# Two gate groups per one-hot instruction, and new homes for the raw chunks of the U table

## The chip, the core and the metric

The kernel runs on one core of one Trainium2 chip. Its engines work side by side, each on its own queue of instructions, and wait for each other by semaphores: TensorE (PE, the matmuls), VectorE (DVE), ScalarE (ACT), GpSimd (POOL) and SyncE (SP, which here only issues transfers). The metric is the device time of one execution in microseconds (us).

## The reference, cut to what matters

The program is one layer of a decoder for 512 tokens of width 1024. A token mixer (Mamba-2 heads beside latent attention, one output projection, a layer norm) comes first and takes the first 390 us. The change lies in what follows, the PEER expert mixer:

```python
def block(xb):                                            # 128 tokens; 4 blocks
    q = (xb @ w_query).reshape(T, 8, 2, 128)
    s = einsum('thkd,hknd->thkn', q, sub_keys)            # scores of 2 x 128 sub-keys per head
    sv, si = top_k(s, 16)
    cand_s = sv[:, :, 0, :, None] + sv[:, :, 1, None, :]  # 256 candidates per head
    top_s, top_pos = top_k(cand_s, 16)
    expert_idx = take(si0 * 128 + si1, top_pos)           # 16 of 16,384 experts per head
    gate = softmax(top_s)
    act = gelu(einsum('td,thkd->thk', xb, u_table[expert_idx]))
    return einsum('thk,thkd->td', gate * act, v_table[expert_idx])
```

then a second layer norm. Each token picks 8 x 16 experts.

## The kernel before

**Dense instead of gathered.** For 352 tokens the kernel does not fetch the chosen rows. It multiplies the tokens with all 16,384 rows of U, in 128 chunks of 128 experts (`u_chunk`, two `step_u` halves of 12 matmuls each; L77 to L79 are the three products of half-precision high and low parts), takes the gelu of each chunk (`act`, L1543), multiplies it by a dense gate matrix G that is zero for the experts not chosen, and multiplies the result with all rows of V. 128 of block 3's and 32 of block 2's tokens are done by gathered rows instead (`row`, L1786, and `urow`, L1302).

**U's chunks.** Each 512 KB chunk is loaded raw by SP (`loads16`, L116), its squares are summed on ACT (`square`, L126, tile `jk`), a tiny matmul and three small ACT steps make a scale from it (`bound`, L132 to L135; for two chunks at a time while the chunk's number f is under FB), ACT writes the high part (`his`, L171), DVE or POOL the low part (`splits`, L191 to L193). Raw chunks lie in a ring of seven buffers: four named `ur`, three in V's low-part buffers `wil`, as long as V's own loads (`wir`) have not begun. The first 18 or so of these chunks are the 16 of `w_query`.

**Routing.** `stage2` computes scores, two top-16 searches per head on DVE, and in `routes` the softmax (an Exp on ACT, L1241) and the digits of the chosen keys (L1254 to L1262). ACT has to load another function table for Exp and again for gelu.

**G (build_g, L1390 to L1488).** 48 gate groups n: three blocks of 128 tokens, 16 groups each. `hot(n)` makes two one-hot arrays on DVE: `oj` (L1403, 128 x 1024) and `gi` (L1406, 128 x 2048, with the gates in it), from digits made every four groups (L1386 to L1388). 16 matmuls (L1433) turn them into G's slices in four PSUM banks, two ACT copies (L1435) put them into `stg`, and every four groups two stores on ACT's queue write them out: `gs0`, 128 KB, and `gsp`, 1920 KB. `oj` and `gi` have two buffers each; `hot(n+1)` is written while the matmuls of n run. Between the groups stand U half-chunks (`step_u`), and in groups 1 to 32 one dot each for the gathered U rows: L1308 on DVE multiplies a gathered row by the token and sums it; then POOL issues the gather of the row three further on (L1302, ring of three `urow` buffers). The order is that of the program text: each engine runs its own instructions as they were issued.

**V.** From chunk 54 on U and V chunks alternate; V's matmuls are L1721, L1722 and L1725, G's slices come back by `gt<-gsp` (L1658).

The change touches `loads16`, `square`'s order in `tick` and `bounds`, `routes`, `hot` and `build_g`, the loop of the output projection after L1470, `u_halves` (L1526) and the step from `build_g` to V (L1650 to L1680).

Of the kernel before, what the change touches and what calls it, by code (L numbers as in the profile page):

```python
# [11 lines left out]
F32 = mybir.dt.float32  # L12
# [37 lines left out]
FB = 72  # L50
# [8 lines left out]
def tile_block(ctx: ExitStack, tc: tile.TileContext, I, out):  # L59
# [25 lines left out]
    class Stream:  # L85
        def __init__(self, p, name, srcs, shape, raw=2, la=1, lo=None, bufs=None):
# [6 lines left out]
            self.sc, self.inv, self.by, self.nq, self.nb = {}, {}, {}, 0, 0  # L93
# [46 lines left out]
        def bounds(self, p, ps):  # L140
            f = self.nb
            if f < len(self.f16) and self.nq > f + (f < FB) and p >= f - ({4: 1, 6: 2, 8: 3}.get(f, 4) if f < FB else 2):
                self.bound(ps())

        def tick(self, p):
            while self.nq < len(self.f16):
                f = self.nq
                if p < ({4: 1, 5: 1, 6: 2, 7: 3, 8: 3, 9: 4}.get(f, f - 6) if f < FB else f - 3.5):
                    break
# [10 lines left out]
        def his(self, m):  # L160
            while self.nh < min(m, len(self.srcs)):
                n = self.nh
                if n in self.fi:
                    if not self.on:
# [15 lines left out]
        def splits(self, m):  # L180
            while self.ns < min(m, len(self.srcs)):
# [5 lines left out]
                if n in self.fi:  # L187
# [7 lines left out]
                    self.loads16(max(min(f + 8, FB), f + 5))  # L195
# [1008 lines left out]
    def routes(pl, ts, po, ti_, nb, nh, dst, after=lambda i: None, room=None, mid2=lambda i: None):  # L1204
# [35 lines left out]
        V.tensor_tensor(ab(1), v4(pf), v4(b1), op=OP.add)  # L1240
        A.activation(f4(d), f4(d), AF.Exp)  # L1241
        yield 0.8 + n * 0.0042
        V.tensor_reduce(sm, g4(d), axis=AX.X, op=OP.add)
        V.reciprocal(sm, sm)
        for i in range(nb):
            V.tensor_tensor(dst(i)[:, 2], d[:, i], sm[:, i * nh:(i + 1) * nh, None].to_broadcast([128, nh, 16]), op=OP.mult)
        yield 0.5 + n * 0.002
        sh = [128, 2 * nh, 16, 16]
        for i in order:
# [9 lines left out]
            yield 0.15 + nh * 0.27  # L1259
            mid2(i)  # L1260
# [131 lines left out]
    def build_g():  # L1392
        def hot(n):
# [3 lines left out]
            if n % 4 == 3:  # L1397
                DG.pop(n - 3)
# [4 lines left out]
            V.tensor_tensor(oj, iotaE[:, None].to_broadcast(bc),  # L1403
                            jT[:, g * 8:g * 8 + 8].rearrange("p (q c) -> p q c", c=2)[:, :, None, :].to_broadcast(bc),
                            op=OP.is_equal)
            V.tensor_tensor(gi.rearrange("p q a e b c -> p (q a) (e b) c"),  # L1406
                            hi[:, q0:q0 + 4].rearrange("p q a c -> p (q a) c")[:, :, None, :].to_broadcast([128, 64, 16, 2]),
# [602 lines left out]
```

## Time and profile before

| | us |
|---|---|
| three runs | 1550.53, 1550.50, 1549.11; median 1550.5 |
| profiled execution, its own time | 1550.87 |
| its span in the trace | 1549.1 (1.8 of the execution lie outside) |
| PE busy in the span | 1519.1 (98%) |
| DVE, ACT, POOL busy | 1346.3, 932.8, 508.1 |

The span runs from the first instruction to the last. PE's busy time is made of matmuls that overlap, so "98%" says that it was seldom without a matmul, not that each ran at its best. The trace names a wait by the engine that waited, what it had to start, and the instruction that released it; stretches below are given in us from the span's start.

### The profile page before, as it was taken

Reading aid. Unit: us, or ns where it says so; the run is one execution under the profiler, and the core shown is the slowest. Engines: PE = TensorE matmul, PEld = TensorE weight load, DVE = VectorE, ACT = ScalarE, POOL = GpSimd, SP = SyncE. Lnnn points to the kernel's source line nnn. Section 1 sums busy time; section 2 is a strip of 40 time slices with the busy share of each in tenths; the row PEclk is TensorE's granted clock in tenths of the full one; section 3 lists DMA queues with packets and bytes.
Section 4 is the critical chain, followed back from the end, with each engine's and each line's share of the span. In section 5 each row is a group of like instructions: output and inputs, shape, how many; then the busy total and the mean of one; then the engine's idle time right before and its main releaser. Section 6 shows DMA issues by size and latency. Waiting matters only on the chain.

```text
span 1549.1 us, 25537 instructions
## 1 busy us (share of the span) xinstructions
PE 1519.1 (98%) x9281; PEld 1162.3 (75%) x9281; DVE 1346.3 (87%) x2609; ACT 932.8 (60%) x1746; POOL 508.1 (33%) x387
## 2 busy tenths in 40 slices
PE   8999999999999999999999999999999999999997
PEld 6787788888677566667777777777777777888886
DVE  8989778837599999999589988999899999999967
ACT  5575566733877887887766666666666664333332
POOL 0000032300144123320043444555555555655400
PEclk9999999999999999999999999999999999999999
DMA  6243132482533469999888999999999999999972
GB/s 251 97 150 103 61 86 77 131 291 78 176 111 97 125 221 341 368 340 293 273 302 324 322 344 323 370 379 388 380 371 378 385 389 327 365 366 355 346 265 89
DMA packets 157887, 404.32 MB, mean 261 GB/s; under 512 B 13800, under 2 KB 66856, under 8 KB 157504
## 3 DMA queue, kind: packets, MB, share of 16 engines
q1 hardware_dynamic: 61072, 212.86, 38.4%
q0 software_dynamic: 45424, 163.73, 28.8%
q10 hardware_dynamic: 51264, 26.09, 5.8%
q8 instruction: 73, 1.20, 0.3%
q14 instruction: 54, 0.44, 0.1%
HBM read 368.33 MB, written 32.19 MB: 259 GB/s over the span
## 4 chain that ended last, share of the span: by engine, by line
PE 84%; DVE 11%; issue 2%; ACT 2%; DMA 1%; SPq 0%; DVEq 0%; ACTq 0%
PE va L1722 11%; PE va L1721 11%; PE va L1725 11%; PE pu L77 8%; PE pu L79 8%; PE pu L78 8%; PE pw L1141 5%; PE pa L77 3%; PE pa L79 3%; PE pa L78 3%; DVE gi L1406 2%; DVE urow L1308 2%; DVE wih L193 1%; DVE oj L1403 1%; PE pw L77 1%
## 5 line engine op out<-in xcount | busy, mean ns | idle before, releaser
L1722 PE MATMUL va<-wil,Ph 128*128 128x512 f32 x726 | 282.9, 390 | 0.0
L77 PE MATMUL pu<-XT,wih 128*128 128x352 f16 x896 | 281.0, 314 | 0.0
L79 PE MATMUL pu<-XT,wih 128*128 128x352 f16 x896 | 280.4, 313 | 0.0
L78 PE MATMUL pu<-XT,wih 128*128 128x352 f16 x896 | 280.3, 313 | 0.0
L1786 POOL DMA_INDIRECT row<-u,ix x128 | 172.4, 1347 | 211.9 <-DVE row L1797 125.3
L1786 POOL DMA_INDIRECT row<-v,ix x128 | 187.3, 1463 | 141.3 <-DVE ac L1813 116.8
L176 ACT ACTIVATE wih<-wir 128x1024 fp32r<-128x1024 f32 (+3 forms) x141 | 142.5, 1011 | 138.6 <-PE va L1725 80.6
L198 DVE TENSOR_TENSOR wil<-wir,wih 128x1024 fp32r<-128x1024 f32 (+1 forms) x121 | 147.1, 1217 | 50.3 <-ACT wih L176 42.2
L1721 PE MATMUL va<-wih,Ph 128*128 128x512 f32 x432 | 172.8, 400 | 0.0
L1813 DVE SCALAR_TENSOR_TENSOR ac<-row,hd,ac 128x1024 f32<-128x1024 f32 x128 | 164.0, 1281 | 7.3 <-DMA row<-v,ix 5.2
L1797 DVE SCALAR_TENSOR_TENSOR row<-row,x 128x1024 f32<-128x1024 f32 x128 | 151.6, 1218 | 11.1 <-DMA row<-u,ix 11.1
L1722 PEld LDWEIGHTS va<-wil,Ph 128*128 128x128 f32 x726 | 136.5, 188 | 25.9
L77 PEld LDWEIGHTS <-wih 128*128 128x128 f16 x920 | 89.8, 98 | 62.4 <-issue 20.6
L1543 ACT ACTIVATE act<-pu,ui 128x352 f32<-128x352 f32 x124 | 68.4, 552 | 107.7 <-PE pu L79 106.9
L1725 PE MATMUL va<-wih,Pl 128*128 128x512 f32 x432 | 133.0, 389 | 0.0
L193 DVE SCALAR_TENSOR_TENSOR wih<-ur,us,wih 128x1024 f16<-128x1024 f32 x97 | 124.4, 1283 | 7.8 <-ACT wih L171 7.8
L79 PEld LDWEIGHTS <-wih 128*128 128x128 f16 x920 | 90.0, 98 | 48.1 <-DVE wih L193 0.5
L126 ACT ACTIVATE jk<-ur 128x1024 bf16<-128x1024 f32 x114 | 119.3, 1047 | 1.5 <-DMA ur<-ut 1.4
L1721 PE MATMUL va<-wihx,Ph 128*128 128x512 f32 x294 | 119.1, 405 | 0.0
L78 PEld LDWEIGHTS <-wih 128*128 128x128 f16 x920 | 90.0, 98 | 37.6
L171 ACT ACTIVATE wih<-ur,us 128x1024 f16<-128x1024 f32 x97 | 110.6, 1140 | 2.9 <-ACT stg L1435 2.0
L176 ACT ACTIVATE wihx<-wir 128x1024 fp32r<-128x1024 f32 x50 | 52.8, 1057 | 78.7 <-PE va L1725 42.8
(559 smaller groups left out, 3534.0 us busy)
## 6 DMA issues: line engine op xcount, KB each, us to landing
wir<-v SPq DMA_DIRECT2D x128, 512.0 KB
ur<-ut SPq DMA_DIRECT2D x105, 512.0 KB
gsp<-stg ACTq DMA_DIRECT2D x12, 1920.0 KB
gt<-gsp SPq DMA_DIRECT2D x30, 768.0 KB
wir<-wo SPq DMA_DIRECT2D x25, 512.0 KB
wil<-ut SPq DMA_DIRECT2D x23, 512.0 KB
wir<-wf SPq DMA_DIRECT2D x18, 512.0 KB
ur<-wqr SPq DMA_DIRECT2D x9, 512.0 KB
```

The source lines that it names most:

```text
L77: T.matmul(ps, lh, rh, start=start, stop=False)
L78: T.matmul(ps, lh, rl, start=False, stop=False)
L79: T.matmul(ps, ll, rh, start=False, stop=stop)
L176: A.activation(h, r, AF.Copy)
L193: V.scalar_tensor_tensor(l, r, self.sc[f][0], h, op0=OP.mult, op1=OP.subtract)
L198: self.lo(n).tensor_tensor(l, r, h, op=OP.subtract)
L1721: T.matmul(va[b][e], Ph[b], h[:, cs], start=c == 0, stop=False)
L1722: T.matmul(va[b][e], Ph[b], l[:, cs], start=False, stop=False)
L1725: T.matmul(va[b][e], Pl[b], h[:, cs], start=False, stop=c == (LASTC if b == 2 and e else 127))
L1786: G.indirect_dma_start(out=R[s], out_offset=None, in_=I["u"] if s < 128 else I["v"], in_offset=bass.IndirectOffsetOnAxis(ap=ix[:, s % 128: ...
L1797: V.scalar_tensor_tensor(r, r, 1.0, x3, op0=OP.mult, op1=OP.mult, accum_out=hd[:, s:s + 1])
L1813: V.scalar_tensor_tensor(ac, r, hd[:, s - 128:s - 127], ac, op0=OP.mult, op1=OP.add)
```

## The change

Lines of the changed kernel lie 6 to 13 higher in this stretch (L1403 is L1410, L1406 is L1413, L1308 is L1315, L193 is L199, L116 is L122, L1241 is L1248).

1. **One-hots of two groups at once.** `oj` becomes 128 x 2048, `gi` 128 x 4096; `hot` is called at even n for n+2. There are still two buffers of each, so they take twice the memory (12 KB more in each partition). The digits of the next four groups are made one group earlier. Three U half-chunks, not two, stand between `hot(0)` and the first matmuls of G.
2. **Raw U chunks.** The four `ur` buffers become one; the chunks with f%7 of 1, 2, 3 use V's raw buffers `wir`, which lie idle until then, and after the gate buffers are closed the last chunks use three new buffers `uv`. The number of buffers in the ring is the same. The load of chunks 71 and on therefore waits for the end of `build_g`; V's first loads are issued one each at n = 45, 46, 47; the last `gsp` store goes behind the last U chunks of the lead.
3. **Bounds.** FB falls from 72 to 70, so one pair of chunks is bounded singly.
4. **routes().** The Exp is issued after a `yield`, and what needs its result (sum, reciprocal, gates) after the first block's first product.
5. **Output projection.** One raw chunk is loaded ahead of it instead of four, the other three behind V's-size items; the squares and bounds stand later; the third U chunk is cut in two around the transposes of block 3.

```diff
-FB = 72
+FB = 70
...
         def loads16(self, m):
+            if self.up is None:
+                m = min(m, FV + 1)
             while self.nf < min(m, len(self.f16)):
                 f, n = self.nf, self.f16[self.nf]
                 if f < FV and f % 7 > 3:
                     t = self.p.tile(self.shape, F32R, name=self.name + "l", bufs=self.bufs).bitcast(F32)
+                elif f < FV and f % 7:
+                    t = self.p.tile(self.shape, F32, name=self.name + "r", bufs=self.rawb)
+                elif f <= FV or f % 4 == 2:
+                    t = self.rp.tile(self.shape, F32, name="ur", bufs=1)
                 else:
-                    t = self.rp.tile(self.shape, F32, name="ur", bufs=4)
+                    t = self.up.tile(self.shape, F32, name="uv", bufs=3)
...
-                    self.loads16(max(min(f + 8, FB), f + 5))
+                    self.loads16(max(min(f + 8, FB), f + (3 if f <= FB else 5)))
...
+        yield 0.8 + n * 0.0042
         A.activation(f4(d), f4(d), AF.Exp)
-        yield 0.8 + n * 0.0042
-        V.tensor_reduce(sm, g4(d), axis=AX.X, op=OP.add)
-        V.reciprocal(sm, sm)
-        for i in range(nb):
-            V.tensor_tensor(dst(i)[:, 2], d[:, i], sm[:, i * nh:(i + 1) * nh, None].to_broadcast([128, nh, 16]), op=OP.mult)
-        yield 0.5 + n * 0.002
...
             V.tensor_tensor(eqv, eqv, tv[:, :, None, :].to_broadcast([128, 32 * nh, 8, 2]), op=OP.mult)
             yield 0.15 + nh * 0.27
+            if i == order[0]:
+                V.tensor_reduce(sm, g4(d), axis=AX.X, op=OP.add)
+                V.reciprocal(sm, sm)
+                for j in range(nb):
+                    V.tensor_tensor(dst(j)[:, 2], d[:, j], sm[:, j * nh:(j + 1) * nh, None].to_broadcast([128, nh, 16]), op=OP.mult)
+                yield 0.5 + n * 0.002
...
-            oj = gb.tile([128, 4, 128, 2], F16, name="oj", bufs=2)
-            gi = gb.tile([128, 4, 16, 2, 8, 2], F16, name="gi", bufs=2)
-            bc = [128, 4, 128, 2]
+            oj = gb.tile([128, 8, 128, 2], F16, name="oj", bufs=2)
+            gi = gb.tile([128, 8, 16, 2, 8, 2], F16, name="gi", bufs=2)
+            bc = [128, 8, 128, 2]
...
         nxt = hot(0)
-        for _ in range(2):
+        for _ in range(3):
             step_u()
...
-            oj, gi = nxt
-            if n < 47:
-                nxt = hot(n + 1)
+            if n % 2 == 0:
+                oj, gi = nxt
+                if n < 46:
+                    nxt = hot(n + 2)
+            if n >= 45:
+                win.cap = len(items)
+                win.loads(win.nl + 1)
...
+            if g == 11 and b < 2:
+                g_head(b + 1)
             if g == 12 and b < 2:
-                g_head(b + 1)
-            if g == 13 and b < 2:
                 g_tail(b + 1)
             if n >= DOT0:
                 next(dots, 0.0)
-            if n % 4 == 2 and n < 44:
-                digits(n + 2)
             if HEAD0 <= n < HEAD0 + 6:
                 next(head, 0.0)
+            if n % 4 == 1 and n < 44:
+                digits(n + 3)
...
-    win.loads16(4)
+    win.loads16(1)
     w_out_step(acc, (1, 2, 0), 9, hl9)
...
     held = {k: item() for k in range(10, 16)}
+    win.loads16(4)
...
+    u2 = u_halves(2, pw)
+    next(u2)
     xt_block(3, xm[3])
-    u_chunk(2, pw)
+    next(u2, None)
...
+    win.up = pool("uv")
+    win.loads16(FV + 2)
...
-    win.cap = len(items)
-    win.loads(win.nl + 3)
     uc = un[0]
     while uc < LEAD:
         u_chunk(uc)
         uc += 1
-        if rest:
-            rest.pop()()
+    rest.pop()()
```

How this moves instructions is shown at three places. First DVE in `build_g`, from the one-hots of group 4 on, in the kernel before (the L1308 rows are the dots of gathered rows 2, 3, 4 and 5; the dot of row 1 stands just ahead):

```order
L1406 TENSOR_TENSOR gi<-dhi,dgl 128x2048
L1308 SCALAR_TENSOR_TENSOR urow,uhd<-urow,ux 128x1024
L193 SCALAR_TENSOR_TENSOR wihx<-wil,us,wihx 128x1024
L1403 TENSOR_TENSOR oj<-iotaE,jT 128x1024
L1406 TENSOR_TENSOR gi<-dhi,dgl 128x2048
L1308 SCALAR_TENSOR_TENSOR urow,uhd<-urow,ux 128x1024
L1403 TENSOR_TENSOR oj<-iotaE,jT 128x1024
L1406 TENSOR_TENSOR gi<-dhi,dgl 128x2048
L1308 SCALAR_TENSOR_TENSOR urow,uhd<-urow,ux 128x1024
L193 SCALAR_TENSOR_TENSOR wih<-wil,us,wih 128x1024
L1403 TENSOR_TENSOR oj<-iotaE,jT 128x1024
L1406 TENSOR_TENSOR gi<-dhi,dgl 128x2048
```

The same engine and place in the changed kernel, from the dots of rows 1 and 2 (one row, x2) to the first one-hot of groups 8 and 9:

```order
L1315 SCALAR_TENSOR_TENSOR urow,uhd<-urow,ux 128x1024 x2
L199 SCALAR_TENSOR_TENSOR wihx<-wil,us,wihx 128x1024
L1410 TENSOR_TENSOR oj<-iotaE,jT 128x2048
L1413 TENSOR_TENSOR gi<-dhi,dgl 128x4096
L1315 SCALAR_TENSOR_TENSOR urow,uhd<-urow,ux 128x1024
L199 SCALAR_TENSOR_TENSOR wih<-wil,us,wih 128x1024
L1315 SCALAR_TENSOR_TENSOR urow,uhd<-urow,ux 128x1024
L1393 TENSOR_TENSOR dhi<-iotaE,dT 128x512
L1394 TENSOR_TENSOR dlo<-iotaE,dT 128x256
L1395 TENSOR_TENSOR dgl<-dlo,gT 128x512
L199 SCALAR_TENSOR_TENSOR wih<-wil,us,wih 128x1024
L1410 TENSOR_TENSOR oj<-iotaE,jT 128x2048
```

Between two dots there was always a one-hot pair of one group; now two dots follow each other, or have only a split (L199) between them, and then comes the work of two groups. The row of dot 4 is gathered into the buffer that dot 1 frees: before, dots 2 and 3, two or three splits, the digits and the one-hots of three groups stood between; now dots 2 and 3, two splits and one pair.

Second ACT around the Exp of `routes` in the kernel before (`dd` is the softmax's tile; each table load serves the row behind it):

```order
L1543 ACTIVATE act<-pu,ui 128x352
L171 ACTIVATE wih<-ur,us 128x1024
L126 ACTIVATE jk,usq<-wil 128x1024
L1214 ACTIVATE tif<-ti 128x8x2x16 x2
L1241 ACT_TABLE_LOAD
L1241 ACTIVATE dd<-dd 128x384
L1543 ACT_TABLE_LOAD
L1543 ACTIVATE act<-pu,ui 128x352
```

and in the changed one:

```order
L1220 ACTIVATE tif<-ti 128x8x2x16 x2
L1555 ACTIVATE act<-pu,ui 128x352
L177 ACTIVATE wih<-wil,us 128x1024
L132 ACTIVATE jk,usq<-ur 128x1024
L1248 ACT_TABLE_LOAD
L1248 ACTIVATE dd<-dd 128x384
L139 ACTIVATE uq<-px 128x2
L140 ACTIVATE us<-uq 128x2
L141 ACTIVATE ui<-uq,sxt 128x2
L1555 ACT_TABLE_LOAD
L1555 ACTIVATE act<-pu,ui 128x352
```

One chunk's gelu, high part and square now stand ahead of the Exp.

Third SP's queue from the end of `build_g` on, before (`ut` is U, `v` V) and after:

```order
L116 DMA ur<-ut 128x1024 x4
L105 DMA wir<-v 128x1024 x3
L116 DMA ur<-ut 128x1024
L105 DMA wir<-v 128x1024
L116 DMA ur<-ut 128x1024
L105 DMA wir<-v 128x1024
```

```order
L122 DMA ur<-ut 128x1024
L105 DMA wir<-v 128x1024 x3
L122 DMA uv<-ut 128x1024 x2
L105 DMA wir<-v 128x1024
L122 DMA uv<-ut 128x1024
L122 DMA ur<-ut 128x1024
```

Four U chunks stood ahead of V's first three loads; now one does, and the next two U loads (71 and 72) follow them, behind the closing of the gate buffers.

## Rows read from the trace of the kernel before

**Rows 1.** PE's waits by releaser, whole span: us in total, times, longest.

```profile
PE pw L1433 <- DVE gi L1406: 9.0, 9, 2.0
...
PE pu L77 <- ACT act L1543: 1.9, 1, 1.9
...
PE pu L79 <- DVE wihx L193: 0.6, 1, 0.6
...
PE px L1157 <- DMA SK<-skT: 0.4, 1, 0.4
```

**Rows 2.** Windows: us, busy PE, PEld, DVE, ACT, POOL; clock, DMA share, GB/s.

```profile
595.00:694.00 99.00, 92.51 (x844) 66.60 (x844) 98.79 (x140) 78.19 (x159) 34.20 (x23) 0.98 1.03 350
...
765.00:1540.00 775.00, 775.00 (x4078) 587.75 (x4076) 700.91 (x1024) 416.45 (x760) 364.00 (x264) 1.00 0.92 341
```

**Rows 3.** The chain of waits, 390 to 745 us: start, us, what held it.

```profile
500.30 0.67 DVE tv L1166 x3
...
578.35 11.33 DMA urow<-u,uix
589.70 1.23 DVE urow L1308 x2
```

**Rows 4.** Groups of DVE instructions by form, 560 to 736 us.

```profile
L1406 DVE TENSOR_TENSOR gi<-dhi,dgl 128x2048 f16<-128x2048 f16 x48 | 58.4, 1217 | 0.0
L1308 DVE SCALAR_TENSOR_TENSOR urow<-urow,ux 128x1024 f32<-128x1024 f32 x32 | 39.0, 1218 | 1.7 <-DMA urow<-u,uix 1.7
```

**Rows 5.** The same view, 410 to 560 us.

```profile
L1254 DVE TENSOR_TENSOR eq<-abf,iaE 128x4096 f16<-128x4096 f16 x3 | 6.8, 2283 | 0.0
```

**Rows 6.** Timeline of DVE, 575 to 612 us: start, us, instruction.

```profile
603.00 1.22 DVE L1308 SCALAR_TENSOR_TENSOR urow<-urow,ux 128x1024 f32<-128x1024 f32 x1
...
604.14 0.69 DVE L1403 TENSOR_TENSOR oj<-iotaE,jT 128x1024 f16<-128x1024 f16 x1
604.75 1.22 DVE L1406 TENSOR_TENSOR gi<-dhi,dgl 128x2048 f16<-128x2048 f16 x1
605.88 1.22 DVE L1308 SCALAR_TENSOR_TENSOR urow<-urow,ux 128x1024 f32<-128x1024 f32 x1
...
608.08 1.28 DVE L193 SCALAR_TENSOR_TENSOR wih<-ur,us,wih 128x1024 f16<-128x1024 f32 x1
609.28 0.69 DVE L1403 TENSOR_TENSOR oj<-iotaE,jT 128x1024 f16<-128x1024 f16 x1
```

**Rows 7.** Timeline of POOL, the gathers of 570 to 612 us.

```profile
596.34 1.74 POOL L1302 DMA_INDIRECT urow<-u,uix  x1 [4.20 <-DVE urow L1308]
...
604.50 1.15 POOL L1302 DMA_INDIRECT urow<-u,uix  x1 [2.34 <-DVE urow L1308]
```

**Rows 8.** Timeline of POOL and DVE, two gathers in V's phase and their dots.

```profile
978.89 0.93 POOL L1786 DMA_INDIRECT row<-u,ix  x1 [0.30 <-issue]
...
987.17 1.23 DVE L1797 SCALAR_TENSOR_TENSOR row<-row,x 128x1024 f32<-128x1024 f32 x1 [0.53 <-DMA row<-u,ix]
...
1110.01 1.16 POOL L1786 DMA_INDIRECT row<-u,ix  x1 [0.30 <-issue]
...
1119.57 1.23 DVE L1797 SCALAR_TENSOR_TENSOR row<-row,x 128x1024 f32<-128x1024 f32 x1 [1.27 <-DMA row<-u,ix]
```

**Rows 9.** Timeline of DVE, 512 to 521 us: the split that L79 waits for.

```profile
518.53 1.28 DVE L193 SCALAR_TENSOR_TENSOR wihx<-ur,us,wihx 128x1024 f16<-128x1024 f32 x1
```

**Rows 10.** Timeline of PE: two of G's waits, and a matmul behind the first.

```profile
594.98 1.38 PE L1433 MATMUL pw<-gi,oj 128*128 128x128 f16 x16 [1.97 <-DVE gi L1406]
...
596.47 0.50 PE L78 MATMUL pu<-XT,wih 128*128 128x352 f16 x1
...
677.50 1.10 PE L1433 MATMUL pw<-gi,oj 128*128 128x128 f16 x16 [1.78 <-DVE gi L1406]
```

**Rows 11.** Timeline of ACT and SP at the step to V.

```profile
745.93 0.37 ACTq L1440 DMA_DIRECT2D gsp<-stg  x1
...
766.00 0.33 SPq L1658 DMA_DIRECT2D gt<-gsp  x1
```

More of the change, by code (lines that the diff above doesn't have):

```diff
@@ L92, in __init__ @@
             self.f16, self.fi, self.nf, self.on, self.wide = [], {}, 0, False, 0
-            self.sc, self.inv, self.by, self.nq, self.nb = {}, {}, {}, 0, 0
+            self.sc, self.inv, self.by, self.nq, self.nb, self.up = {}, {}, {}, 0, 0, None
         def halves(self, ns):
@@ L141, in bounds @@
             f = self.nb
-            if f < len(self.f16) and self.nq > f + (f < FB) and p >= f - ({4: 1, 6: 2, 8: 3}.get(f, 4) if f < FB else 2):
+            if f < len(self.f16) and self.nq > f + (f < FB) and p >= f - ({4: 1, 6: 2, 8: 3}.get(f, 4) if f < FB + 1 else 2):
                 self.bound(ps())
@@ L147, in tick @@
                 f = self.nq
-                if p < ({4: 1, 5: 1, 6: 2, 7: 3, 8: 3, 9: 4}.get(f, f - 6) if f < FB else f - 3.5):
+                if p < ({4: 1, 5: 1, 6: 2, 7: 3, 8: 3, 9: 4}.get(f, f - 6) if f <= FB else f - 2 if f == FB + 1 else f - 3.5):
                     break
@@ L163, in his @@
                 if n in self.fi:
-                    if not self.on:
+                    if not self.on or self.fi[n] not in self.sc:
                         return
@@ L1396, in hot @@
             hi, lo, gl = DG[n // 4 * 4]
[L1397 to L1398 removed]
+            if n % 4 == 2:
+                DG.pop(n - 2)
             q0 = g % 4 * 4
[L1400 to L1402 removed]
+            oj = gb.tile([128, 8, 128, 2], F16, name="oj", bufs=2)
+            gi = gb.tile([128, 8, 16, 2, 8, 2], F16, name="gi", bufs=2)
+            bc = [128, 8, 128, 2]
             V.tensor_tensor(oj, iotaE[:, None].to_broadcast(bc),
[L1404 removed]
+                            jT[:, g * 8:g * 8 + 16].rearrange("p (q c) -> p q c", c=2)[:, :, None, :].to_broadcast(bc),
                             op=OP.is_equal)
             V.tensor_tensor(gi.rearrange("p q a e b c -> p (q a) (e b) c"),
[L1407 to L1408 removed]
+                            hi[:, q0:q0 + 8].rearrange("p q a c -> p (q a) c")[:, :, None, :].to_broadcast([128, 128, 16, 2]),
+                            gl[:, q0:q0 + 8].rearrange("p q e b c -> p q (e b c)")[:, :, None, :].to_broadcast([128, 8, 16, 32]),
                             op=OP.mult)
@@ L1429, in build_g @@
                 for t in range(4):
-                    q, c = hf * 2 + t // 2, t % 2
+                    q, c = n % 2 * 4 + hf * 2 + t // 2, t % 2
                     pt = ps[:, t * 128:(t + 1) * 128].rearrange("p (a b) -> p a b", b=8)
@@ L1492, in tile_block @@
             win.square(0)
-            win.square(1)
-        if b in (1, 2):
+        if b == 2:
+            win.bound(px())
             win.bound(px())
@@ L1500, in tile_block @@
         if b == 1:
-            win.square(2)
-            win.square(3)
+            for f in (1, 2, 3):
+                win.square(f)
     close(hold)
@@ L1535, in u_halves @@
                 yield
-                win.bounds(win.fi[cn] + (win.fi[cn] < 4), lambda: (px() if win.fi[cn] < FB - 4 else last[0])[:, NU:NU + 2])
+                win.bounds(win.fi[cn] + (win.fi[cn] < 4), lambda: (pw() if cn < win.f16[4] else px() if win.fi[cn] < FB - 4 else last[0])[:, NU:NU + 2])
         last[0] = bank
@@ L1840, in tile_block @@
             xv = [xf[:, j * 1024:j * 1024 + 1024] for j in range(3)] + [pool("xq").tile([128, 1024], F32R, name="xq")]
-            xv += [xt.tile([128, 1024], F32R, name="ur", bufs=4) for _ in range(4)]
+            xv += [xt.tile([128, 1024], F32R, name="ur", bufs=1)]
+            xv += [win.up.tile([128, 1024], F32R, name="uv", bufs=3) for _ in range(3)]
             win.place = {i0 + j: (xv[2 * j], xv[2 * j + 1]) for j in range(4)}
```

1 line of the change is left out of this document (removed).

## The prediction

> **What bounds the kernel now.** I read PE's waits first. The nine waits of G's matmuls for `gi` make 9.0 us; gelu and split at 519 us cost 1.9 and 0.6, and one load of sub-keys 0.4 [rows 1]. There is little else to win on PE. The windows say where these waits arise: from 595 to 694 us PE is busy for 92.51 of 99 us, DVE for 98.79, and the DMA share is 1.03 at 350 GB/s, while from 765 to 1540 us PE is busy for all of 775 us [rows 2]. So in `build_g` DVE sets the pace, and from the end of `build_g` PE does; what the change is worth is how much earlier or later DVE brings the last one-hots that PE waits for. That is group 40: from there on the matmuls follow without a wait for `gi`, and the same matmuls remain in both kernels. The chain of waits agrees: DVE is on it from 500.30 on, and the only thing that stopped DVE on the way is one gather of a U row, 11.33 us from issue to dot [rows 3]; the wait it made on DVE was 1.7 us, the only one of 32 dots [rows 4].
>
> **Part 1, the one-hots.** Start to start, `oj` of one group takes 604.75 - 604.14 = 0.61 us and `gi` 605.88 - 604.75 = 1.13, together 1.74 [rows 6]. A product of 128x4096 in the same type lasts 2.283 us [rows 5] and one of 128x2048 1.217 [rows 4]; since 0.08 us of the latter's 1.217 lies under the next start, I price the double `gi` at 2.20 and the double `oj`, which has `gi`'s old size, at 1.13. A pair is 3.34 against 3.48. In front of G40's matmuls stand 41 groups now, 41 x 1.74 = 71.3 us; afterwards 21 pairs, which include group 41, 21 x 3.34 = 70.1. That is -1.2 us. If the pair saved nothing it would be 21 x 3.48 - 71.3 = +1.8; if the whole fixed part of 0.15 us by duration (2 x 1.217 - 2.283) fell away twice per pair, -4.5. I take -1.2, the nearest rows.
>
> In the Trainium skill, "Perfetto Trace Analysis", section "Optimizing Scalar/DVE Operations", grouping helps a saturated engine, but breaking instructions up may let work finish sooner when an engine leaves bubbles on another. By its first half the sum is as above; by its second half the sum is the +1.8 bound, since G40 then also waits for group 41. DVE's 98.79 of 99 us is the first case.
>
> **Part 1, the dots.** This is what I think decides. In front of the change the dots are a group apart; the gather of 596.34 was not waited for although its dot came only 605.88 - 596.34 = 9.54 us later [rows 6, 7]. POOL issues a gather 1.50 us after the start of the dot three rows earlier (604.50 against 603.00) [rows 6, 7]. Afterwards dots come in twos. From the start of dot 1 to that of dot 4 stand dots 1, 2 and 3 (3 x 1.14, as 604.14 - 603.00), two splits (2 x 1.20, as 609.28 - 608.08 [rows 6]) and one pair, 3.34. That is 9.17 us, and less the 1.50 it leaves 7.68 from issue to dot (with unrounded parts). So it is for rows 4, 8, 16, 20 and 24; with small other work in between rows 12 and 28 have 8.15; for rows 6, 10 and 14 dots 3, 4 and 5, two splits, the pair and the three digit instructions (608.08 - 605.88 - 1.14 = 1.06) stand between, which gives 8.72. The rest has 9.9 or more. What does a gather need? Before shows only "not over 9.54" and 11.33. Gathers of the same 4 KB rows in V's phase, where the dot was waiting and the landing is thus seen, took 987.17 - 978.89 = 8.28 and 1119.57 - 1110.01 = 9.56 us [rows 8], at 341 GB/s, much the same load as 350 [rows 2]. Then DVE gets new waits, whose sum over the build I call W. At 8.28 for all: 5 x 0.60 + 2 x 0.13 = 3.3. At the mean of the two, 8.92: 5 x 1.24 + 2 x 0.77 + 3 x 0.20 = 8.3. At 7.68 or less: 0. If all took 9.56: 14.7. I take 4.6, that is 8.28 for most and one gather 1.3 us longer, since a gather that collides with the store of G is the exception in before as well. The old wait of 1.7 us is part of W now, so it goes out of the sum: -1.7. Behind a waiting dot on DVE stand a split that the next half-chunk needs and the one-hots of two groups, so W passes to PE in full as long as DVE sets the pace.
>
> **The clock.** The matmul wait of 1.97 us at 594.98 was followed by matmuls of 0.50 instead of 0.31 us: TensorE ran at 1.2 instead of 2.4 GHz for a while; the wait of 1.78 at 677.50 was not followed by this [rows 10]. The granted clock over 595 to 694 was 0.98, so such a stretch costs about 0.02 x 99 = 2.0 us of PE work [rows 2], most of which the next wait for DVE absorbs. New waits of DVE gather PE's waiting in fewer, longer pieces, at one G of every four. Only a fall near G40 shows at the end: 0 to 2.0; I take 0.7.
>
> **Part 4, the Exp.** Without Exp and its table loads ahead of it the gelu at 518 us frees its bank 1.9 us earlier, but L79, one product later, needs the split that runs on DVE from 518.53 to 519.81 [rows 9], and DVE, not PE, is the chain there [rows 3]. So the 1.9 us turn into a wait for the split and nothing is won: 0. Were the split early too, PE would still wait at the first G. What now stands between Exp and its users on DVE is a product of 2.28 us [rows 5]; if the Exp came later than that, DVE would lose what is over, and I allow 0 to 1.0 us of loss.
>
> **Parts 3 and 5.** A third U chunk, cut in two, puts 12 matmuls ahead of block 3's transposes and frees a raw buffer a little sooner; I give it the wait for the sub-keys, 0.4 [rows 1], because the scores start DVE's chain: -0.4, between -2.0 (if the other small waits around 400 us go as well) and +0.5. The single bound adds one matmul of two columns and three ACT steps, under 0.1 us on engines with room.
>
> **Part 2, the raw chunks.** Seven buffers in the ring before and after, with the same order of freeing; in `build_g` this costs nothing. At the step to V two U loads wait for the gate buffers, three V loads go ahead of them, and the last 1920 KB store, issued at 745.93, goes behind two more chunks, some 7 us later. At 341 GB/s it would take 5.8 us alone and up to the 16 us between two stores when shared, so it ends by 769 at the latest, and the load that reads it back is issued at 766.00 [rows 2, 11]. PE has V's chunks to do then. I take 0, ends 0 and 3.
>
> **The sum.** -1.2 - 1.7 - 0.4 + 4.6 + 0.7 = +2.0 on the profiled execution's 1550.87 (span 1549.1 and 1.8 outside): 1552.9. That execution lies 0.4 above the median of the runs, so I forecast 1552.5 us, for itself between 1550 and 1555 (W from 2 to 7).
>
> **Rivals.**
> A. Gathers land in time: they take 7.7 us or less in `build_g`, so W is 0 to 1.5 (0.75) and no clock falls. -3.3 + 0.75 = -2.5: 1548.3 profiled, 1547.9 by the median. For it: 31 of 32 dots did not wait, and their gathers may have landed long before their dots. Against it: both landings that are seen in V's phase are later than 7.68, and so is the one seen here.
> B. Slower: gathers need as much as 8.92 us on the average in every four groups, W is 8.3 and two clock falls show with 1.5: -3.3 + 9.8 = +6.5, or 1557.4, 1557.0 by the median. It decides from about 8.6 us on. For it: DMA share of 1.03 and a gather of 11.33 us that was issued just behind a store. Against it: V's phase has gathers of 8.28 at the same traffic.
> C. The step to V stalls PE for 2 us (late chunk 71 or G slices): 1554.5.
> D. The pair doesn't do what it says: DVE gains nothing because the stores, 1920 KB every four groups at a DMA share over 1, hold the PSUM evictions and with them the matmuls to the old 16 us, or because the double instruction saves nothing and G40 waits for group 41 too (the skill page's second half). Then the -1.2 becomes 0 to +1.8: 1553.7 to 1555.5 with W, 1551 without it; I count 1551.
>
> **How the numbers follow.** Chances: forecast 0.45, A 0.22, B 0.20, C 0.07, D 0.06. 0.2% (3.1 us) is what a measurement of this kernel can tell from no change. Faster than 1547.4 is half of A and a little of the rest, 0.16. Slower than 1553.6 is B, most of C and the upper quarter of the forecast, 0.37. Within: 0.47. The range takes A and B nearly to their ends, with the unknowns of parts 4 and 5: 1546.5 to 1558.
>
> **What would show it.** Right: in the profile after, waits of DVE's L1315 for the gathered row at rows 4, 8, 16, 20, 24, 0.3 to 2 us each; `gi` of 128x4096 near 2.28 us; PE's waits for `gi` at every fourth group and in sum above 9.0; the wait at 518 us turned from gelu to split. Wrong: dots without waits (then A), a PE wait between 741 and 770 us (C), `gi` well over 2.3 us or the third ACT eviction of every four waiting for the store (D). The forecast falls if these waits of DVE make under 2 us or over 7 in all.

## The result and the profile after

| | before | changed |
|---|---|---|
| median of the runs, us | 1550.5 (6 runs, 1549.1 to 1558.6) | 1568.2 (6 runs, 1564.0 to 1568.7) |
| span of the profiled execution, us | 1549.1 | 1566.0 |

The ratio is 1.0104, with a 95% interval from 1.0087 to 1.0121: slower, by about one per cent. The forecast was 1552.5, in a range up to 1558; the time lies outside.

PE's waits in the changed kernel, in the columns of [rows 1] (releaser, us in total, times, longest):

```profile
PE pw L1444 <- DVE gi L1413: 17.9, 8, 4.7
...
PE pu L79 <- DVE wihx L199: 2.7, 1, 2.7
PE px L1344 <- DVE uw L1340: 2.1, 1, 2.1
PE va L1734 <- ACT Ph L1718: 1.9, 1, 1.9
```

The wait for the one-hots has doubled, from 9.0 us. At 519 us the waits for gelu and split of before, 1.9 and 0.6, have become one of 2.7 for the split. The last two rows are new.

The windows of [rows 2], and the one that follows the first of them (columns: us, busy PE, PEld, DVE, ACT, POOL; clock, DMA share, GB/s):

```profile
595.00:694.00 99.00, 84.69 (x784) 62.01 (x785) 90.66 (x107) 66.81 (x134) 31.84 (x23) 0.98 1.01 328
694.00:741.00 47.00, 41.27 (x383) 29.74 (x381) 43.88 (x51) 39.08 (x82) 4.22 (x5) 0.96 0.87 270
```

DVE was busy for 98.79 of these 99 us; now it stands still for 8.3 of them. Doing less was not its problem. What stopped it, in its groups between 560 and 760 us (columns as in [rows 4]: busy, mean ns | idle before, releaser):

```profile
L1413 DVE TENSOR_TENSOR gi<-dhi,dgl 128x4096 f16<-128x4096 f16 x24 | 54.8, 2282 | 0.0
L1315 DVE SCALAR_TENSOR_TENSOR urow<-urow,ux 128x1024 f32<-128x1024 f32 x32 | 38.7, 1218 | 12.4 <-DMA urow<-u,uix 12.4
L1410 DVE TENSOR_TENSOR oj<-iotaE,jT 128x2048 f16<-128x2048 f16 x24 | 29.4, 1223 | 3.4 <-PE px L138 2.5 <-PE pw L1444 0.8
```

The double one-hots cost what was forecast (2282 ns; 24 of them 54.8 us against 58.4 for 48 single ones [rows 4]). The dots wait 12.4 us for their rows. The seven waits are those of rows 4, 8, 12, 16, 20, 24 and 28. Four of them, with the issue of their gathers on POOL and two stores of G on ACT's queue, from the timeline of these engines (start, us, [idle before <-releaser]):

```profile
576.75 0.67 ACTq L1451 DMA_DIRECT2D gsp<-stg  x1
...
577.78 1.68 POOL L1309 DMA_INDIRECT urow<-u,uix  x1 [5.80 <-DVE urow L1315]
...
589.51 1.23 DVE L1315 SCALAR_TENSOR_TENSOR urow<-urow,ux 128x1024 f32<-128x1024 f32 x1 [3.94 <-DMA urow<-u,uix]
...
597.74 1.68 POOL L1309 DMA_INDIRECT urow<-u,uix  x1 [5.79 <-DVE urow L1315]
...
606.71 1.23 DVE L1315 SCALAR_TENSOR_TENSOR urow<-urow,ux 128x1024 f32<-128x1024 f32 x1 [1.18 <-DMA urow<-u,uix]
...
629.98 0.68 ACTq L1451 DMA_DIRECT2D gsp<-stg  x1
...
632.45 1.68 POOL L1309 DMA_INDIRECT urow<-u,uix  x1 [5.79 <-DVE urow L1315]
...
643.53 1.23 DVE L1315 SCALAR_TENSOR_TENSOR urow<-urow,ux 128x1024 f32<-128x1024 f32 x1 [3.30 <-DMA urow<-u,uix]
...
686.41 1.74 POOL L1309 DMA_INDIRECT urow<-u,uix  x1 [5.79 <-DVE urow L1315]
...
694.95 1.22 DVE L1315 SCALAR_TENSOR_TENSOR urow<-urow,ux 128x1024 f32<-128x1024 f32 x1 [0.32 <-DMA urow<-u,uix]
```

Read them as pairs. 589.51 - 577.78 = 11.73 us from issue to dot, and 3.94 of that is waiting, so the lead was 7.79. The gather was issued 1.0 us behind a store of 1920 KB; so was that of 632.45 (2.5 us behind, 11.08 us). The other two were issued over 5 us behind a store and took 8.97 and 8.54.

Where the 17 us arise is seen in instructions that both kernels have. G's matmuls of groups 38 and 40, in the kernel before and then in the changed one:

```profile
712.37 1.09 PE L1433 MATMUL pw<-gi,oj 128*128 128x128 f16 x16
...
718.55 1.09 PE L1433 MATMUL pw<-gi,oj 128*128 128x128 f16 x16
```

```profile
721.97 1.09 PE L1444 MATMUL pw<-gi,oj 128*128 128x128 f16 x16
...
727.93 0.24 PE L1344 MATMUL px<-ident,uw 32*128 32x32 f32 x1 [2.13 <-DVE uw L1340]
...
728.32 0.50 PE L78 MATMUL pu<-XT,wihx 128*128 128x352 f16 x1
...
731.54 1.13 PE L1444 MATMUL pw<-gi,oj 128*128 128x128 f16 x16
```

That is +9.6 us at group 38 and +13.0 at group 40. The last gelu before V's first product starts at 762.61 instead of 749.51 (+13.1), and one of the first gelus of V's phase at 793.30 instead of 776.38 (+16.9); from there to the end the distance stays.

The +3.4 in the middle is a small step of the gathered tokens' gates. PE's transpose waits 2.13 us for a product of 0.27 us (L1340), which now stands on DVE behind a whole pair of one-hots; then the matmuls run at 0.50 instead of 0.31 us, at 1.2 instead of 2.4 GHz.

The last +3.9 arises at the step to V. In the changed kernel and then in the kernel before, the last 128 KB store of G (`gs`), the U loads beside it, the load that reads it back (`gt`) and its first use:

```profile
753.62 1.69 SPq L122 DMA_DIRECT2D uv<-ut  x2
754.23 0.37 ACTq L1450 DMA_DIRECT2D gs<-stg  x1
...
759.69 1.12 POOL L1674 DMA_DIRECT2D gt<-gs  x2 [36.90 <-DMA uv<-ut]
...
766.96 0.52 DVE L1701 TENSOR_TENSOR gt<-act,gt 128x352 f32<-128x352 f32 x1 [8.83 <-DMA gt<-gs]
```

```profile
742.01 0.37 ACTq L1439 DMA_DIRECT2D gs<-stg  x1
742.35 0.33 SPq L116 DMA_DIRECT2D ur<-ut  x1
...
744.52 1.11 POOL L1658 DMA_DIRECT2D gt<-gs  x2 [31.52 <-ACT wihx L176]
...
749.90 0.53 DVE L1688 TENSOR_TENSOR gt<-act,gt 128x352 f32<-128x352 f32 x1 [4.73 <-PE pu L79]
```

From store to read-back it takes 5.46 us instead of 2.51, and from there to the use 7.27 instead of 5.38, when two U loads have started 0.6 us ahead of the store. The traces also keep the semaphore events by which a transfer tells that it has landed. By them the store landed 4.71 us after its issue instead of 1.85, and the read-back followed 0.75 and 0.66 us later: the store was late, whatever releaser the rows name for the read-back.

### The profile page after: what moved, and what is told of

The parts are those of the page before. It is cut to its first block, busy times and chain, and to the rows that moved or that the text cites. A ratio compares the mean times of both kernels' runs of the same rounds, so it can differ in the third digit from the quotient of the medians.

```text
span 1566.0 us, 25482 instructions
## 1 busy us (share of the span) xinstructions
PE 1522.1 (97%) x9282; PEld 1164.5 (74%) x9282; DVE 1343.8 (86%) x2561; ACT 933.3 (60%) x1749; POOL 507.0 (32%) x387
## 4 chain that ended last, share of the span: by engine, by line
PE 83%; issue 6%; DVE 5%; ACT 2%; POOL 2%; DMA 2%; ACTq 0%; DVEq 0%; POOLq 0%; SPq 0%
PE va L1734 11%; PE va L1735 11%; PE va L1738 11%; PE pu L77 8%; PE pu L79 8%; PE pu L78 8%; PE pw L1147 5%; PE pa L77 3%; PE pa L79 3%; PE pa L78 3%; POOL urow L1309 2%; PE pw L79 1%; PE pw L77 1%; PE pw L78 1%; PE px L1163 1%
## 5 line engine op out<-in xcount | busy, mean ns | idle before, releaser
L79 PE MATMUL pu<-XT,wih 128*128 128x352 f16 x896 | 280.1, 313 | 0.0
L1799 POOL DMA_INDIRECT row<-u,ix x128 | 178.3, 1393 | 208.8 <-DVE row L1810 126.4
L1799 POOL DMA_INDIRECT row<-v,ix x128 | 182.3, 1424 | 145.8 <-DVE ac L1826 120.7
L79 PEld LDWEIGHTS <-wih 128*128 128x128 f16 x920 | 89.8, 98 | 48.8 <-DVE wih L199 1.4
L1734 PEld LDWEIGHTS va<-wih,Ph 128*128 128x128 f32 x432 | 81.2, 188 | 17.4
L1738 PEld LDWEIGHTS va<-wih,Pl 128*128 128x128 f32 x432 | 81.1, 188 | 17.1
L1738 PE MATMUL va<-wihx,Pl 128*128 128x512 f32 x294 | 91.3, 392 | 0.0
```

Of the source, the lines that this page charges most:

```text
L79: T.matmul(ps, ll, rh, start=False, stop=stop)
L1734: T.matmul(va[b][e], Ph[b], h[:, cs], start=c == 0, stop=False)
L1738: T.matmul(va[b][e], Pl[b], h[:, cs], start=False, stop=c == (LASTC if b == 2 and e else 127))
L1799: G.indirect_dma_start(out=R[s], out_offset=None, in_=I["u"] if s < 128 else I["v"], in_offset=bass.IndirectOffsetOnAxis(ap=ix[:, s % 128: ...
```

## The experiments

Where nothing else is said, an edit starts from the changed kernel, and medians are compared with 1568.2. The kernel before, run again beside each group of experiments, had medians of 1549.8 to 1550.9, so medians of different groups compare to about 1 us.

**e1_spread: dots spread around the double one-hots.**

```diff
             if n % 2 == 0:
                 oj, gi = nxt
+                if 2 <= n <= 32:
+                    next(dots, 0.0)
                 if n < 46:
                     nxt = hot(n + 2)
...
-            if n >= DOT0:
+            if n >= 2 and n % 2 == 0 or n > 32:
                 next(dots, 0.0)
```

> The changed kernel with its dots placed otherwise: both dots of a pair of groups are issued at the even group, one ahead of the double one-hots and one behind, so that no gather has only one pair of one-hots between its issue and its dot. Nothing else differs. Theory (short leads meet gathers that need 9 to 12 us behind a store of G): DVE's waits for gathered rows fall from 12.4 us to between 0 and 3, and the time falls by 9 to 11, to about 1558 us (1556 to 1560). Rival 1 (the double one-hots or the stores set the pace, and the gather waits only fill time that would be lost anyway): PE's waits for gi stay near 18 us and the time stays at 1564 to 1568. Rival 2 (gathers are slow because two are under way at once): spreading halves the waits, about 1562.

1553.8 us (10 runs, 1551.8 to 1558.4), ratio to before 1.0016 (1.0000 to 1.0032): 14.4 us gone, more than the 9 to 11 expected. DVE's wait for rows and the window of 595 to 694 us:

```profile
DVE urow L1315 <- DMA urow<-u,uix: 0.8, 1, 0.8
```

```profile
595.00:694.00 99.00, 92.94 (x860) 67.36 (x858) 98.79 (x119) 77.28 (x158) 40.60 (x24) 1.00 1.03 356
```

12.4 us of waits have become 0.8 and DVE is busy throughout, with the double one-hots still there. PE's wait for `gi` is 6.0 us, under the 9.0 of before, and G's matmuls of group 38 start at 709.28, 3.1 us earlier than in the kernel before. Rival 1 is out. Rival 2 (two gathers under way at once) is not tested by this, since the longer leads hide a slow gather as well; f3_ring2 bears on it. The gain is larger than the waits, since no half-rate stretch follows them here (clock 1.00): the wait of 2.1 us for `uw` is still there, but from group 38 to group 40 it costs 1.8 us, not 3.4, with the matmuls behind it at 0.31 us, and those behind the wait at V's start take 0.39 us where the changed kernel's take 0.63.

**e2_head: the gates' small steps ahead of the one-hots.**

```diff
                 oj, gi = nxt
+                if HEAD0 <= n < HEAD0 + 6:
+                    next(head, 0.0)
...
-            if HEAD0 <= n < HEAD0 + 6:
+            if n % 2 and HEAD0 <= n < HEAD0 + 6:
                 next(head, 0.0)
```

> The changed kernel with the steps of the gathered tokens' gates (L1340 among them) issued ahead of the double one-hots at even groups instead of behind. Theory (PE's transposes at 728 us wait 2.1 us because the small scaling stands behind 3.3 us of one-hots on DVE, and the clock falls after it): that wait goes, the half-rate stretch at 728 us with it, and the time falls by 2 to 4 us, to about 1565. Rival (DVE is late there anyway, so that the next gi takes over the wait): no change, 1568.

1566.2 us (1565.3 to 1566.5): 2.0 less, as the theory has it, though these four runs lie inside the changed kernel's 1564.0 to 1568.7, so the time alone does not show it. The trace does: the wait for `uw` is gone, PE's wait for `gi` rose from 17.9 to 18.2 only, and G's matmuls of group 40 start at 728.10 instead of 731.54. The wait at V's start, 2.7 instead of 1.9, takes a part back.

**e3_gt: U chunks 71 and 72 loaded by POOL behind the read-back.**

```diff
-                nc.sync.dma_start(t, self.srcs[n])
+                (G if f in (FV + 1, FV + 2) and self.up is not None else nc.sync).dma_start(t, self.srcs[n])
...
-    win.loads16(FV + 2)
     gt = {}
...
     for q in range(2):
         load_g(q)
+    win.loads16(FV + 3)
```

> The changed kernel with the loads of U chunks 71 and 72 into the new buffers issued by POOL behind the two loads of G's first slices, instead of by SP as soon as the gate buffers are closed. Theory (1 MB of U loads issued 0.6 us ahead of the last 128 KB store of G holds that store up, and the load that reads it back comes 2.5 to 3 us late, so that the first V matmul waits 1.9 us and the clock falls once more): the load of G's first slices is issued about 2.5 us after the store, as in the kernel before (744.52 against 742.01), the wait of 1.9 us and the half-rate stretch at 769 go, and the time falls by 2.5 to 4 us, to about 1564.5. Rival (the load of the slices itself is slow beside other loads): it is issued earlier but lands no earlier, gain under 1 us.

1574.6 us, 6.4 more: a miss in the time, though half of the theory held. The read-back was issued 2.7 us after its store (754.60 to 757.28) and used 4.7 us later, but

```profile
PE pu L138 <- ACT jk L132: 7.3, 1, 7.3
```

the squares of chunk 71, which stand on ACT ahead of V's first steps, now wait for the late load, and PE for them.

**e4_single: one-hots of one group each.** `build_g` as before (with the V loads at n = 45 to 47), all else changed.

```diff
-            oj = gb.tile([128, 8, 128, 2], F16, name="oj", bufs=2)
-            gi = gb.tile([128, 8, 16, 2, 8, 2], F16, name="gi", bufs=2)
+            oj = gb.tile([128, 4, 128, 2], F16, name="oj", bufs=2)
+            gi = gb.tile([128, 4, 16, 2, 8, 2], F16, name="gi", bufs=2)
...
-            if n % 2 == 0:
-                oj, gi = nxt
-                if n < 46:
-                    nxt = hot(n + 2)
+            oj, gi = nxt
+            if n < 47:
+                nxt = hot(n + 1)
```

> The changed kernel with build_g as in the kernel before: one-hots group by group, digits, gate heads, dots and half-chunks in the old order; the new homes of the raw chunks, the Exp, the output projection's and the step to V stay as changed. Theory (merging the one-hots makes the gather waits and the late head, 10.7 and about 3 us; the step to V costs 3.8; the early edits give 0.7): about 1553.5 us (1551 to 1555), with one or no wait for a gather and the wait at V's start still there. Rival (the new homes of the raw chunks slow build_g, for instance since loads of raw chunks come later): 1560 or more, with gather waits still near 12 us.

1553.0 us (1551.5 to 1554.4), as expected. Gather waits 1.6 us; PE is 0.4 us ahead of before through all of G, so the new homes of the raw chunks cost nothing in `build_g`, and PE's wait for `uw` is not there; at V's start PE waits 2.2 us.

**f1_spread_head: e1 and e2 together.**

> The changed kernel with the dots spread around the double one-hots (as in e1_spread) and the steps of the gathered gates ahead of them (as in e2_head). Theory (at 715 us PE waits 2.1 us for a small step behind 3.3 us of one-hots; with DVE no longer late by the gathers nothing else takes the wait over): 2 us less than e1_spread's 1553.8, about 1552. Rival (the wait for the last gi at 704 us grows by as much, since G's one-hots come later by the steps put in front): same as e1_spread.

1554.2 us (1550.4 to 1560.9): a miss, nothing won. The first of the steps now waits on DVE, ahead of the one-hots, for a load that comes after the last dot:

```profile
DVE uw L1333 <- DMA uw<-ugh: 5.3, 1, 5.3
```

The last dot stands as far ahead of this step as in e2, but its results go out to memory and come back, and from the issue of that store to the use it took 12.6 us here (697.93 to 710.48), 9.7 in f2 and 8.0 in e2, where DVE waited 2.5 and 0.7 us. The profile is that of the longest of the twelve runs.

**h1_spread_scale: e1 with only L1340 ahead of the one-hots.**

```diff
                 oj, gi = nxt
+                if n == HEAD0 + 2:
+                    next(head, 0.0)
...
-            if HEAD0 <= n < HEAD0 + 6:
+            if HEAD0 <= n < HEAD0 + 6 and n != HEAD0 + 2:
                 next(head, 0.0)
```

> e1_spread with only the one small scaling of the gathered gates (L1340, group 38) issued ahead of the double one-hots; the steps before it, which wait for a load, stay where the changed kernel has them. Theory (f1_spread_head lost because the first of these steps, put ahead of the one-hots at group 36, waits 2.5 to 5.3 us for its load; the wait of PE's transposes is due to L1340 alone): no wait for the load, PE's wait of 2.1 us at 715 us goes, 1.5 to 2 us under e1_spread, about 1552. Rival (the next gi takes the wait over): same as e1_spread, 1553.8.

1551.6 us, ratio 1.0001 (0.9991 to 1.0011): 2.2 under e1, as expected, though the two ratios' intervals overlap. The wait for `uw` is gone, and group 40 starts 1.7 us earlier than in e1 (715.55 against 717.22). G's matmuls of group 44 start 3.0 us earlier than before (728.25 against 731.25) and the gelu ahead of V's first product 2.9; at V's start a wait of 2.0 us with a half-rate stretch takes it back.

**f2_spread_head_gt0 and f4_single_gt0: only the first slice read back at the step** (f2 from f1, f4 from e4).

```diff
-    for q in range(2):
-        load_g(q)
+    load_g(0)
```

> f1_spread_head, and POOL loads only the first of the two 768 KB slices of G at the step to V; the second follows when the first V chunk is prepared. Theory (the first slice lands 8 us after DVE could use it because it shares the DMA engines with the second one and three 512 KB loads): the first slice lands 2 to 3 us earlier, PE's wait of 1.4 us for it goes, and the time is 1.5 to 2 us under f1_spread_head, about 1550. Rival (the slice is late because its last 128 KB store is held up by the U loads in front of it): no gain, or under 0.5 us.

> e4_single (the changed kernel with one-hots of one group each) and only the first slice of G loaded at the step to V. Theory: its PE wait of 2.2 us at 755 us goes with the earlier landing, and the time falls from 1553.0 to about 1551 (with 0.4 us of early gain and what other waits at the step remain). Rival (the U chunks that can be loaded only after the gate buffers are closed set the step): no change, 1553.

1555.8 and 1553.0 us: misses both, no gain; PE still waits 2.5 and 2.0 us. But the edit did not take the second slice away. V's preparation of its first chunk asks for it at once, and POOL issues the two 0.57 us apart, as in f1:

```profile
745.60 1.11 POOL L1678 DMA_DIRECT2D gt<-gs  x2 [32.95 <-DMA uv<-ut]
```

So these two runs say nothing of what the second slice does to the first; that stays untested.

**h2_spread_scale_u72: from h1, only chunk 72 behind the read-back**, and its squares behind V's first two ACT steps.

> h1_spread_scale, and at the step to V only U chunk 71 is loaded ahead of G's first slices; chunk 72 is loaded by POOL behind them, and its squares go behind the first two ACT steps of V. Theory (the last 128 KB store of G is held up by the two U loads, 512 KB each, that start just ahead of it; e3_gt freed the store but put the square of chunk 71 in front of ACT's V steps): the load of the slices is issued 3 to 4 us after the store instead of 5, they land 1.5 to 3 us earlier, PE's wait at V's start of 1.4 to 3.7 us goes below 1, and the time is 1 to 3 us under h1_spread_scale, about 1550. Rival (one load ahead holds the store as two do, or chunk 72 is then late): no gain, or a new wait of PE for chunk 72's scale.

1558.3 us: a miss. One U load ahead of the store (737.51 against 738.12) does as much as two: the read-back comes after 5.1 us, as in h1, and is used 7.1 us later; and chunk 72's squares are late, with 7.7 us of waiting on PE.

**f3_ring2: the kernel before with two gather buffers.**

```diff
-            UR[n] = ug.tile([128, D], F32, name="urow", bufs=3)
+            UR[n] = ug.tile([128, D], F32, name="urow", bufs=2)
...
-            ug_fetch(n + 3)
+            ug_fetch(n + 2)
```

> The kernel before with two buffers for gathered U rows instead of three, so that each gather is issued two dots ahead instead of three; one-hots stay single and nothing else differs. Leads from issue to dot fall from about 10.5 us to about 6.5. Theory (a gather of the build needs 7 to 11 us from issue to dot, the longest behind a store of G, whatever the one-hots look like): nearly every dot waits, 1 to 4.5 us each, 40 to 90 us in all, and the time rises by 20 to 80 us. Rival (gathers are slow in the changed kernel only because they are issued in twos): leads of 6.5 us would do for most, and the time stays within 8 us of the kernel before.

1571.7 us, ratio 1.0129 (1.0112 to 1.0147). With single one-hots, too, shorter leads cost what the dots wait:

```profile
DVE urow L1308 <- DMA urow<-u,uix: 20.7, 8, 5.3
```

20.7 us of waits, +21.9 us of time. The rival is out: gathers are issued singly here, and those that are waited for still took 7.5 to 10.8 us. The size was under the 40 to 90 expected: only eight dots wait, about one in each stretch of four groups, for gathers issued 2 to 9 us behind a store of 1920 KB, while the 14 issued over 13 us behind one were all in time after 6.5 to 7.7 us. Gathers are long behind a store, not throughout.

**h3_early: the kernel before with the later Exp and the new order of the output projection.** The edits are those of the change, parts 4 and 5.

> The kernel before with the changed routes() (Exp later) and the changed order of the output projection and of the third U chunk; raw buffers, one-hots and the step to V as before. Theory: PE is ahead by 0.4 to 0.7 us up to the start of build_g, as in the changed kernel, the wait at 518 us turns from the gelu to the split, and 0.5 to 1 us remain at the end, about 1549.5, not to be told from the kernel before. Rival (DVE meets build_g with the gathers and stores in another phase, and one wait for a gather more or less decides): up to 1.7 us either way.

1550.3 us, ratio 0.9995 (0.9985 to 1.0004): the same, as expected; PE is 0.5 us ahead up to group 36. Its profiled execution was its longest (1559.6 of 1549.0 to 1559.6). It falls 2.6 us behind by group 40, after DVE has waited 3.0 us for the load of `uw`, and loses the rest at the step to V:

```profile
743.47 0.33 SPq L116 DMA_DIRECT2D ur<-ut  x1
743.84 0.37 ACTq L1440 DMA_DIRECT2D gs<-stg  x1
...
749.02 1.11 POOL L1662 DMA_DIRECT2D gt<-gs  x2 [33.40 <-PE pu L79]
...
758.69 0.53 DVE L1692 TENSOR_TENSOR gt<-act,gt 128x352 f32<-128x352 f32 x1 [10.96 <-DMA gt<-gs]
```

The old step, but here the U load started 0.37 us ahead of the store: 5.2 and 9.7 us instead of 2.5 and 5.4, and PE waits 4.1 us. In the profile of before it started 0.34 us behind. The kernel before has long runs as well (up to 1558.6); whether they come about in the same way is not shown, since none of them was profiled.

**i1_spread_scale_store and i2_store: the U loads behind the store, on the store's own queue** (i1 from h1, i2 from the changed kernel).

```diff
-                nc.sync.dma_start(t, self.srcs[n])
+                (A if f in (FV + 1, FV + 2) else nc.sync).dma_start(t, self.srcs[n])
...
-    win.loads16(FV + 2)
+    win.loads16(FV + 3)
```

> h1_spread_scale, with U chunks 71 and 72 loaded by ACT's queue behind the last 128 KB store of G, instead of by SP just ahead of it. In all runs so far in which a U load starts before that store (by 0.1 to 0.7 us), the read-back is issued 4.4 to 5.5 us after the store and its result used 7 to 9.7 us later; in the two in which the store goes first, it is 2.5 and 2.7, and 5.4 and 4.7. Theory (who goes first decides): 2.5 to 3 us from store to read-back, 5 to 6 from there to the first use, PE's wait for V's first product under 0.5 us instead of 2.0 and no half-rate stretch at 753 us; the time falls from 1551.6 to 1547 to 1549, under the kernel before. Rival (the U loads, now 1 to 2 us later, are late themselves, as in h2_spread_scale_u72): PE waits for the scale of chunk 71, and nothing is won.

> The changed kernel, with the same single edit: U chunks 71 and 72 loaded by ACT's queue behind the last store of G. Theory: the 1.9 us wait at V's start and the half-rate stretch behind it go, 3 to 4 us less than the changed kernel's 1568.2, about 1564.5; the gather waits of 12 us and the late scaling at 728 us stay. Rival: no change or a wait for chunk 71's scale.

i1: 1548.0 us (11 runs, 1547.5 to 1548.4), ratio 0.9984 (0.9975 to 0.9993): faster than both kernels. i2: 1563.3 us (1562.8 to 1565.7), 4.9 under the changed kernel, more than the 3 to 4 expected. Of the 5.0 us between the two profiles 3.8 arise at the step to V, the other 1.2 earlier, where the edit changes nothing. The step to V in i1:

```profile
738.05 0.37 ACTq L1454 DMA_DIRECT2D gs<-stg  x1
739.43 0.86 ACTq L122 DMA_DIRECT2D uv<-ut  x2
...
740.86 1.11 POOL L1678 DMA_DIRECT2D gt<-gs  x2 [30.61 <-DMA gs<-stg]
...
748.11 0.53 DVE L1705 TENSOR_TENSOR gt<-act,gt 128x352 f32<-128x352 f32 x1 [5.45 <-DMA gt<-gs]
```

The read-back is issued 2.8 us after the store. To its first use it takes 7.2 us, more than the 5 to 6 expected, perhaps since the U loads run beside it; but it is in time, and PE has no wait there in either kernel. The runs of i1 also spread over 1.0 us only, those of h1 over 5.9; that the order is the reason is not shown, since i2, which sets it too, spread over 2.9 in four runs.

In the Trainium skill, "DMA: Bandwidth & Descriptors", section "Queues, rings and completion order", each DMA engine takes turns between the queues that have work, a packet at a time. That two queues share is what the trace shows: a small store lands 2 to 3 us late beside a load on another queue that began 0.4 to 0.6 us earlier. It does not show by itself why being 0.34 us ahead is enough to be spared.

## Why the prediction was wrong

**The waits for gathered rows (W): the step that failed.** Its place, its cause and its leads were right: the waits came at rows 4, 8, 16, 20, 24 and at 12 and 28, and the leads, worked out as 7.68 and 8.15, measured 7.75 to 7.79 and 8.22 to 8.25. Rows 6, 10 and 14 had no wait, because the wait of a row just ahead made their 8.72 longer (to 9.8 and more). The size was wrong: 12.4 us against 4.6, over the 7 at which the forecast was to fall. I had set the time from issue to dot at "8.28 for most", from gathers of V's phase, where no store of G runs. In `build_g` the seven took 8.35 to 11.73, 9.68 in the mean. The row that told of this stood in the prediction: the 11.33 us in the kernel before, which I took for an exception. Its gather was issued 2.2 us behind a store of the kernel before:

```profile
576.20 0.69 ACTq L1440 DMA_DIRECT2D gsp<-stg  x1
```

In the changed kernel the short leads fall again and again to gathers that are issued there. That such gathers are the long ones is seen in the rows (11.73, 11.08 and 9.82 at 1.0 to 2.5 us behind a store; 8.35 to 9.27 at 5 to 6.5), and in the semaphore events for all gathers, waited for or not: in the two kernels together the 12 issued 0.5 to 5 us behind a store landed after 8.7 to 12.0 us, the 13 issued 13 us or more behind one after 4.4 to 8.7. What I called the exception was the rule for that place, in the kernel before too. No run took the stores away, so that the store itself makes the gather long is not shown beyond this. e1 and f3 show that the waits, from either side, are what the time pays for: at group 38 the changed kernel is 12.4 us behind h1, whose waits for rows are 0.8 us. Rival B had this mechanism with 8.92 us.

**The one-hots: right.** h1 has them and is 3.0 us ahead of before at group 40; -1.2, the old wait of 1.7 and the early edits' 0.4 to 0.7, less h1's own wait of 0.8, make 2.5 to 2.8. A part of the gain is lost on the way: between groups 34 and 36 the changed kernel, e1 and h1 each lose 2.0 us to a wait of 1.8 for a pair of which PE needs only the first group, and e4, with single one-hots, loses none.

**What was missing: the small step behind the pair.** The prediction asked for what waits behind a waiting instruction, and not for what waits behind a longer one: L1340, 0.27 us long, 2.1 us late, with a half-rate stretch 3.4 us in all from group 38 to group 40. The second half of the Trainium skill's rule ("Perfetto Trace Analysis", "Optimizing Scalar/DVE Operations") is to break instructions up where ScalarE or VectorE aren't saturated but leave bubbles on other engines. It bears on this place: from 694 to 741 us DVE was busy for 43.88 of 47 us, not for 98.79 of 99, and with the pairs broken up again, in e4, the wait is gone. I had weighed it at G40 alone. Moving the step ahead of the pair does it too, in e2 and h1: PE reaches group 40 3.4 us earlier than in the changed kernel and 1.7 earlier than in e1, and the medians fall by 2.0 and 2.2.

**The step to V: a term of 0 that was 3.9.** Rival C had its place and 2 us, for another reason (chunk 71 or G's slices late through the last 1920 KB store). What happened is that the U loads, which the change lets go when the gate buffers close, start 0.6 us ahead of the last 128 KB store of G. i2, which puts them behind it, loses 0.1 us at this step instead of 3.9, of which 1.9 was PE's wait and 1.6 came behind it at the lower clock.

**The clock.** I had 0.7 us, for a fall near G40. One came there, behind the wait for `uw`: the same wait of 2.1 us costs 1.8 us in e1, where the matmuls behind it run at 2.4 GHz, and 3.4 in the changed kernel, where they run at 1.2; so 1.6 us there, and 1.6 more behind the wait at V's start (span +16.9 against +15.3 at V's first product). Over 595 to 694 us the granted clock is 0.98 in both kernels.

**The Exp and the early edits: right.** The 1.9 us became a wait for the split; 0.7 us remained of 0.4 expected, and h3 cannot be told from before.

So +16.9 is made of +9.6 up to group 38 (W less the old wait is 10.7, and the one-hots and the early edits give some of it back), +3.4 and +3.9. Against the forecast's +2.0, W was 7.8 too small, the small step and the step to V were left at nothing, and the clock's 0.7 is contained in these two: 2.0 + 7.8 + 3.4 + 3.9 - 0.7 = 16.4.

## What to carry to other kernels

Merging instructions on a saturated engine moves everything that stood between them: before pricing the saving, list each instruction whose buffer is refilled, or whose result another engine awaits, between the merged ones, and compare its new lead with the longest latency that the trace has for that transfer in that stretch, not with the usual one elsewhere. Small steps that another engine awaits go ahead of the long ones, unless they wait themselves. Where a short store is on the way to a read-back, loads issued beside it on another queue can go behind it on its own queue, if they can wait that long: i1 and i2 gained by this, while in e3 and h2, which put loads behind the read-back, a square came late by it and cost more than was won.

## What was not expected of the hardware

A 128 KB store and a 512 KB load that start within 0.4 us of each other on two queues give two outcomes, by which comes first: the store's reader could go 2.5 us after the store when the store was 0.34 us ahead (before), and 5.2 us when the load was 0.37 us ahead (h3). In all other profiles too the reader went after 2.6 to 2.8 us where the store came first and after 4.4 to 5.5 where a load did.
